# Seven block products for 20 instead of 16 FFN blocks, and two instead of four FFN blocks ahead of the sampled tokens

## The chip, the core and the metric

The kernel runs on one core of a Trainium2 chip. A core has TensorE (PE in the profile; its weight loads are PEld), VectorE (DVE), ScalarE (ACT), GpSimd (POOL) and SyncE (SP), which here only issues DMAs. Each engine works through its own instructions in a fixed order and waits on semaphores. TensorE reads SBUF and accumulates in PSUM, which has eight banks. The metric is the device time of one execution in microseconds (us).

## The reference

One layer of a decoder step for 1024 prompt tokens and 64 sampled tokens (8 sequences of 8), width 1024, all in float32:

```python
shift1, scale1, gate1, shift2, scale2, gate2 = mod
mix, states = mixer(rmsnorm(x, g_mix) * (1 + scale1) + shift1)
x = x + gate1 * (mix @ w_out)
x = x + gate2 * swiglu(rmsnorm(x, g_ffn) * (1 + scale2) + shift2, w_gate_up, w_down)
```

`swiglu` computes `(silu(gate) * up) @ w_down` with 2816 hidden columns. The mixer is a short convolution, a dilated window attention and a window attention; for the sampled tokens it reads key and value caches of up to 2048 positions per sequence. A final RMS norm follows. The outputs are the tokens and the updated caches.

## The kernel before

**Layout.** Activations lie transposed: 128 channels on the partitions, the 1088 tokens along the free axis, in three groups (`GRP`): 366, 366 and 356 tokens. The 64 sampled tokens are the end of the third, "group 2". A row buffer (`row`, 11 of them) holds 128 channels of all tokens, an `act_tile` (3 of them) holds all 1024 channels of one group, split in two halves.

**Every large matmul is three.** To keep float32 accuracy, `halves` (L85) splits a weight tile of 128 x 512 into a high half (ScalarE, L90) and a low half (VectorE, at times GpSimd, L91), and activations are split in the same way. `mm3` (L199) then issues three matmuls for each 128 x 128 block: L205 high by high, L206 high by low, L207 low by high. Weights arrive through SP's queue into five `wraw` buffers and are split into four `wsp` buffers. `gemm` (L217) multiplies one output block: two weight tiles, and for each group 8 x 3 = 24 matmuls.

**The order of the work.** The program is written in one order, and a planner places each instruction on its engine by readiness in its own timing of the program; earlier code has precedence. After the attention of the prompt the code goes on:

- `sample_steps` (L714) is the attention of the sampled tokens. It streams the caches through seven `raw` buffers: scores (L661), minimum, exponential, transposes, weighting of the values (L695). It stops nine times, and at each stop two steps of `ahead_steps` (L879) are issued: splitting the mix of groups 0 and 1, the output projection `w_out` of these groups (eight steps), the norm (`second_rstd`, `second_norm`), then `gate_up` of the FFN blocks 0 to 3 for groups 0 and 1, each with one modulation tile (`late_mod`), and the eight steps of their down projection. Six of these come after the last stop.
- The "mid" stage: the mix of group 2 is split (`split_mix`, L612), `w_out` of group 2 is computed for eight output blocks, then its norm (`rstd` L784, with the broadcast matmuls L801 into a bank of the kind "s"; `second_norm` L810), and `gate_up` of blocks 20 and 21 for groups 0 and 1.
- The "ffn" stage: group 2 of blocks 0 to 3, with one `sums_step` (L955) behind each; their down projection for group 2; then pairs of blocks, (20, 21), (4, 5) and so on to (18, 19), each pair with its down projection into the residual rows `x1` (`add_gated`).
- The tail: the last pair's down projection, the final norm and the output, over other token ranges (`LAST`).

**Seven products.** `gate_up_2x2` (L968) computes gate and up for groups 0 and 1 as one 2 x 2 block product: the weights' blocks are gate and up by the two halves of the 1024 input channels, the activations' blocks the two groups by the same halves. Instead of eight products of blocks it computes seven, from sums of weights (`t1` to `t4`, on GpSimd, four `tw` buffers) and sums of activations (`SA`, made once by four calls of `sums_step`: on GpSimd L947, then VectorE and ScalarE). A product is 4 x 3 = 12 matmuls of 366 columns. Group 2 of the block is multiplied plainly (`third`). Banks: the products take those of the kinds "s" (two) and "t" (two), plain gates those of kind "g" (three).

**Caches.** The updated caches are copied by 38 DMAs, DRAM to DRAM, from ScalarE's queue; `next_copy` issues the next of them behind a given instruction.

## Time and profile before

| | us |
|---|---|
| median of 3 runs | 1411.46 |
| lowest, highest | 1411.25, 1416.62 |
| profiled execution | 1411.32 |
| its span | 1409.5 |

The profile is of one execution. Its span runs from the first instruction of the program to the last; the execution's own time has 1.8 us more around it. A row of a window shows, for each engine, the time it was busy and how many instructions (x) it ran, then the granted share of TensorE's clock, the share of the DMA engines' time and the GB/s moved. Matmuls overlap in the pipeline, so a matmul's own duration is longer than what it adds; the spacing of starts is what counts. A group's row gives line, engine, operation, output and inputs with their shapes, the count, then busy us and mean ns, then the engine's idle time before it and who ended it.

### The profile page before, as it was taken

How to read it: one execution, taken by the hardware profiler on the slowest of the kernel's cores; microseconds unless marked ns; L12 is line 12 of the kernel's file. 1: busy time of each engine (PE TensorE's matmuls, PEld its weight loads, DVE VectorE, ACT ScalarE, POOL GpSimd, SP SyncE). 2: the span in 40 equal slices, each digit the busy share in tenths (PEclk: the TensorE clock that was granted, in tenths of full speed). 3: DMA queues.
4: the chain of work that ended last, by engine and by line, in shares of the span. 5: the costliest groups of instructions: out<-in, count | busy, mean ns of one | idle time of the engine just before them, and what ended most of it. 6: DMA issues, size and time to landing. Idle time of an engine off the chain costs nothing.

```text
span 1409.5 us, 23915 instructions
## 1 busy us (share of the span) xinstructions
PE 1353.3 (96%) x9097; PEld 1286.7 (91%) x9097; DVE 841.0 (60%) x1935; ACT 582.5 (41%) x1204; POOL 329.1 (23%) x364
## 2 busy tenths in 40 slices
PE   7999999999999998998998999999999999999994
PEld 5889999979898887888998999999999999999994
DVE  5468768265775326214569665757565666665657
ACT  5398764465654325222344413131313232322243
POOL 2143343233335220102015020202021111111114
PEclk9999999999999999999999999999999999999997
DMA  9342421452416679875333513141515142423103
GB/s 361 107 160 99 135 99 29 128 191 90 143 31 218 208 251 331 280 253 169 112 123 103 143 45 120 30 165 45 186 31 187 51 159 68 144 87 130 44 30 128
DMA packets 100804, 190.81 MB, mean 135 GB/s; under 512 B 14048, under 2 KB 51456, under 8 KB 100096
## 3 DMA queue, kind: packets, MB, share of 16 engines
q1 hardware_dynamic: 94112, 135.67, 30.1%
q10 hardware_dynamic: 6416, 53.55, 10.6%
q8 instruction: 72, 1.18, 0.3%
q14 instruction: 44, 0.36, 0.1%
q0 software_dynamic: 160, 0.04, 0.0%
HBM read 181.22 MB, written 59.23 MB: 171 GB/s over the span
## 4 chain that ended last, share of the span: by engine, by line
PE 83%; DMA 7%; DVE 4%; issue 2%; POOL 1%; ACT 1%; SPq 0%; POOLq 0%; ACTq 0%; DVEq 0%
PE ps_g L205 18%; PE ps_g L207 18%; PE ps_g L206 18%; PE ps_s L206 3%; PE ps_s L205 3%; PE ps_s L207 3%; DMA wraw<-in_w_gu 3%; PE ps_o L579 3%; PE ps_t L206 2%; PE ps_t L205 2%; PE ps_t L207 2%; PE ps_t L570 2%; DMA raw<-in_bv 1%; PE ps_g L180 1%; PE ps_s L528 1%
## 5 line engine op out<-in xcount | busy, mean ns | idle before, releaser
L205 PE MATMUL ps_g<-act,wsp 128*128 128x366 f32 (+1 forms) x1192 | 400.0, 337 | 5.5 <-ACT wsp L90 3.3
L207 PE MATMUL ps_g<-act,wsp 128*128 128x366 f32 (+1 forms) x1192 | 396.0, 333 | 4.0 <-DVE wsp L91 3.9
L206 PE MATMUL ps_g<-act,wsp 128*128 128x366 f32 (+1 forms) x1192 | 397.7, 334 | 0.4 <-DVE act L617 0.4
L90 ACT ACTIVATE wsp<-wraw 128x512 fp32r<-128x512 f32 x232 | 145.3, 629 | 270.5 <-PE ps_g L207 170.4
L205 PEld LDWEIGHTS ps_g<-act,wsp 128*128 128x128 f32 x1192 | 227.6, 191 | 13.0 <-issue 5.5
L207 PEld LDWEIGHTS ps_g<-act,wsp 128*128 128x128 f32 x1192 | 227.1, 191 | 9.2 <-DVE wsp L91 5.0
L91 DVE TENSOR_TENSOR wsp<-wraw,wsp 128x512 fp32r<-128x512 f32 x194 | 144.5, 745 | 146.3 <-ACT wsp L90 141.5
L206 PEld LDWEIGHTS ps_g<-act,wsp 128*128 128x128 f32 x1192 | 227.8, 191 | 4.0 <-issue 2.5
L205 PE MATMUL ps_g<-hid,wsp 128*128 128x366 f32 (+3 forms) x464 | 152.7, 331 | 4.6 <-DVE ts L767 3.6
L206 PE MATMUL ps_g<-hid,wsp 128*128 128x366 f32 (+3 forms) x464 | 152.3, 328 | 1.7 <-DVE hid L852 1.7
L207 PE MATMUL ps_g<-hid,wsp 128*128 128x366 f32 (+3 forms) x464 | 152.6, 329 | 0.0
L972 POOL TENSOR_TENSOR tw<-wraw 128x512 f32<-128x512 f32 x16 | 21.8, 1365 | 322.9 <-DMA wraw<-in_w_gu 157.0
L205 PEld LDWEIGHTS ps_g<-hid,wsp 128*128 128x128 f32 x464 | 87.6, 189 | 7.2 <-issue 3.6
L90 ACT ACTIVATE wsp<-tw 128x512 fp32r<-128x512 f32 x64 | 40.5, 633 | 122.5 <-PE ps_g L207 59.3
L206 PE MATMUL ps_s<-act,wsp 128*128 128x366 f32 x272 | 90.2, 332 | 0.0
L205 PE MATMUL ps_s<-act,wsp 128*128 128x366 f32 x272 | 90.1, 331 | 0.0
L206 PEld LDWEIGHTS ps_g<-hid,wsp 128*128 128x128 f32 x464 | 87.9, 189 | 2.5 <-DVE hid L852 2.3
L207 PE MATMUL ps_s<-act,wsp 128*128 128x366 f32 x272 | 89.9, 330 | 0.0
L91 POOL TENSOR_TENSOR wsp<-wraw,wsp 128x512 fp32r<-128x512 f32 x38 | 49.9, 1313 | 169.6 <-ACT wsp L90 158.0
L207 PEld LDWEIGHTS ps_g<-hid,wsp 128*128 128x128 f32 x464 | 87.8, 189 | 0.0
L763 DVE SCALAR_TENSOR_TENSOR p_qc<-ps_g,MOD,p_qc 128x366 f32<-128x366 f32 (+3 forms) x99 | 56.5, 572 | 39.9 <-PE ps_g L207 38.0
L763 DVE SCALAR_TENSOR_TENSOR p_q<-ps_g,MOD,p_q 128x366 f32<-128x366 f32 (+3 forms) x99 | 55.3, 570 | 38.5 <-PE ps_g L207 38.5
(346 smaller groups left out, 2453.3 us busy)
## 6 DMA issues: line engine op xcount, KB each, us to landing
wraw<-in_w_gu SPq DMA_DIRECT2D x112, 256.0 KB, 2.7
wraw<-in_wmod SPq DMA_DIRECT2D x64, 256.0 KB, 3.6
raw<-in_bk SPq DMA_DIRECT2D x30, 512.0 KB, 7.8
raw<-in_bv SPq DMA_DIRECT2D x30, 512.0 KB, 8.4
out_bk_b<-in_bk ACTq DMA_DIRECT2D x12, 1016.0 KB, 7.3
wraw<-in_w_in SPq DMA_DIRECT2D x36, 256.0 KB, 5.4
wraw<-in_w_d SPq DMA_DIRECT2D x36, 256.0 KB, 2.6
mraw<-in_wmod SPq DMA_DIRECT2D x32, 256.0 KB, 5.2
```

The lines of the kernel that those rows point to most:

```text
L90: S.activation(sp[:, 0, :], raw, AF.Copy)
L91: (V if not state["sub"] or state["n"] % state["sub"] else G).tensor_tensor(sp[:, 1, :], raw, sp[:, 0, :].bitcast(F32), op=OP.subtract)
L180: ins = PE.matmul(ps[32 * q:32 * q + 32, :256], lhsT=csil[:, 4 * hf + q, :], rhs=raws[2 * hf + q // 2][:, q % 2 * 256:q % 2 * 256 + 256], ...
L205: PE.matmul(ps[:, :n], lhsT=w_hi, rhs=a(0, ak), start=first and j == 0, stop=False, **kw)
L206: PE.matmul(ps[:, :n], lhsT=w_hi, rhs=a(1, ak), start=False, stop=False, **kw)
L207: PE.matmul(ps[:, :n], lhsT=w_lo, rhs=a(0, ak), start=False, stop=last and j == m - 1, **kw)
L528: PE.matmul(ps[:, :sn], lhsT=QH[:, qsl], rhs=KS[hd][:, kk], start=True, stop=False)
L570: PE.transpose(pt[:, col:col + 128], Sb[:, (kb - k0) * 128:(kb - k0 + 1) * 128], ident)
L579: PE.matmul(po[:, q0:q0 + w], lhsT=Vt[:, kb, hd].rearrange("p a b -> p (a b)"), rhs=PT[:, hl, c0:c0 + w], start=fresh, stop=ch is chunks[- ...
L763: ins = V.scalar_tensor_tensor(x1[m][:, c0:c0 + k], ps[:, :k], MOD[:, gate + m, 0:1], x1[m][:, c0:c0 + k], op0=OP.mult, op1=OP.add)
L972: G.tensor_tensor(t1, b12, b11, op=OP.subtract)
```

## The change

`FF_GROUPS` becomes two lists. Ahead of the sampled tokens stand the blocks 0 and 1 only; blocks 2 and 3 join the late pairs, and all late pairs, (20, 21) among them, are computed by seven products.

```diff
-FF_GROUPS = ((0, 4), (20, 2)) + tuple((f, 2) for f in range(4, 20, 2))
+FF_AHEAD = (0,)
+FF_PAIRS = (20,) + tuple(range(2, 20, 2))
```

The down weights are now stored for pairs alone, so the ahead blocks' down projection is four steps of one weight tile instead of eight; with this the ahead steps are 18 instead of 24. The modulation tiles move from the gate steps to every second projection step:

```diff
         for m in range(KC):
             w_out(m, (0, 1))
+            late_mod(m % 2)
             yield
...
-                late_mod(1)
```

The mix of group 2 goes into an `act_tile` instead of a tile of the mid stage, and is split before the memory of the sampled tokens is given back. The early constants' memory is given back before the mid stage, and the buffers of the sums (`tw`, `SA`) are taken from there on:

```diff
+    mx[2] = act_tile()
+    split_mix(2, mx[2])
     samp.close()
...
     early_pool.close()
...
+    sp_ = sums.enter_context(tc.tile_pool(name="sums", bufs=1, reuse_waits="tile"))
```

The mid stage holds the sums and the seven products of blocks 20 and 21, without their group 2 (`hh` is `None`), which stays where it was:

```diff
+        for m in range(KC):
+            w_out(m, (2,))
+            if m % 2:
+                sums_step(m // 2)
+        second_norm(2, second_rstd(2))
+        first = [row("u_ff") for _ in range(NPRE)]
+        for f, u in enumerate(first):
+            gate_up_2x2(FE + f, u, None)
```

In the ffn stage, group 2 of blocks 0 and 1 is computed without sums, and blocks 2 and 3 become the second pair. `gate_up_2x2` issues two cache copies instead of one for the blocks below 6 and in the mid stage:

```diff
+        for _ in range(2 if f < 6 or hh is None else 1):
             next_copy(ins)
```

In the tail, the buffers of the final norm (accumulator, broadcast row, three temporaries) lie in one tile that takes the place of the sum `sa1`, instead of a pool of their own.

More of the change, by code (lines that the diff above doesn't have):

```diff
@@ L912, in _build @@
     late_mod(16)
+    mx[2] = act_tile()
+    split_mix(2, mx[2])
     samp.close()
-    FE = FF_GROUPS[1][0]
-    with tc.tile_pool(name="mid", bufs=1) as mid:
-        scratch["ff"] = mid
-        state["sub"] = 0
-        mx[2] = mid.tile([128, 2, KC, 366], F32R, name="mx2")
-        split_mix(2, mx[2])
-        for m in range(KC):
-            w_out(m, (2,))
-        second_norm(2, second_rstd(2))
-        first = [row("u_ff") for _ in range(NPRE)]
-        for f, u in enumerate(first):
-            gate_up(FE + f, u, None, (0, 1))
@@ new lines, in gate_up_2x2, with product, third @@
+    def gate_up_2x2(f, u, hh):
+        c2, n2 = GRP[2]
+        b11, b12, b22, b21 = [load(d["w_gu"][f, n, hf]) for n, hf in ((0, 0), (1, 0), (1, 1), (0, 1))]
+        t1, t2, t3, t4 = [tw() for _ in range(4)]
+        G.tensor_tensor(t1, b12, b11, op=OP.subtract)
+        G.tensor_tensor(t2, b22, t1, op=OP.subtract)
+        G.tensor_tensor(t3, b22, b12, op=OP.subtract)
+        G.tensor_tensor(t4, b21, t2, op=OP.subtract)
+        uv = row("uv")
+        u2, u3 = uv[:, 0:N2], uv[:, N2:2 * N2]
+        g0, g1, g2 = [u[:, c:c + n] for c, n in GRP]
+        def product(ps, w, a, first):
+            mm3(ps, w, [(k, k) for k in range(4)], a, N2, first=first, more=not first)
+        def third(ps, w, half, first):
+            if hh is not None:
@@ new lines, in gate_up_2x2 @@
+        pd = ps_tile("s")
+        product(pd, wsel(halves(t3)), lambda hl, k: SA[3][:, hl, k, :], True)
+        V.tensor_tensor(u3, u2, pd[:, :N2], op=OP.add)
+        w = wsel(halves(b21))
+        product(pa, w, lambda hl, k: h2[0][:, hl, 4 + k, :], False)
+        ins = S.activation(g0, pa[:, :N2], AF.Silu)
+        third(pg, w, 1, False)
+        if hh is not None:
+            ins = S.activation(g2, pg[:, :n2], AF.Silu)
+        pe = ps_tile("t")
+        product(pe, wsel(halves(t1)), lambda hl, k: SA[1][:, hl, k, :], True)
@@ L1015, in gate_up_2x2 @@
+        V.tensor_tensor(g0, g0, u2, op=OP.mult)
+        if hh is not None:
             split_hid(u, hh, 0, N2)
```

188 lines of the change are left out of this document (81 added, 107 removed).

## The prediction

> **What bounds the kernel now.** I read the page first (engine shares, chain), then the busy time by stage around the places that change, then the rows that price single operations.
>
> ```profile
> span 1409.5 us, 23915 instructions
> PE 1353.3 (96%) x9097; PEld 1286.7 (91%) x9097; DVE 841.0 (60%) x1935; ACT 582.5 (41%) x1204; POOL 329.1 (23%) x364
> ...
> PE 83%; DMA 7%; DVE 4%; issue 2%; POOL 1%; ACT 1%; SPq 0%; POOLq 0%; ACTq 0%; DVEq 0%
> ```
>
> TensorE is the bound: 83% of the chain. The remainder sits in a few stages, so next the stretches from the start of the sampled tokens to the first late pair, and one steady late pair:
>
> ```profile
> core 0: us, PE busy (x) PEld busy (x) DVE busy (x) ACT busy (x) POOL busy (x), PEclk, DMA share, GB/s
> 442.00:546.00 104.00, 97.44 (x1016) 83.34 (x1015) 37.11 (x103) 37.36 (x70) 26.85 (x51) 0.97 0.79 257
> 546.00:650.70 104.70, 96.91 (x815) 86.42 (x813) 29.02 (x61) 29.79 (x53) 10.63 (x10) 0.93 0.78 265
> 650.70:679.30 28.60, 28.60 (x175) 28.54 (x172) 17.25 (x35) 8.66 (x24) 5.58 (x7) 1.00 0.39 116
> 679.30:710.70 31.40, 31.40 (x195) 31.40 (x194) 19.43 (x39) 13.08 (x23) 4.78 (x5) 1.00 0.45 126
> 710.70:744.20 33.50, 33.50 (x205) 33.50 (x205) 21.92 (x64) 16.31 (x34) 7.64 (x12) 1.00 0.38 127
> 744.20:781.80 37.60, 33.74 (x194) 32.85 (x193) 33.21 (x53) 18.61 (x38) 16.10 (x12) 0.95 0.39 112
> ...
> 1156.00:1224.50 68.50, 68.13 (x409) 67.58 (x409) 42.83 (x83) 19.06 (x35) 10.47 (x9) 1.00 0.32 109
> ```
>
> By the code these are: 442 to 650.7 sampled tokens, interleaved with the "ahead" steps; 650.7 to 679.3 the six down steps left of them, under which the mix of group 2 is split; 679.3 to 710.7 the output projection of group 2 (192 matmuls); 710.7 to 744.2 its norm, under which TensorE computes 192 products of blocks 20 and 21; 744.2 to 781.8 group 2 of blocks 0 to 3 (192 matmuls) together with the sums for the seven products; the last row is one pair of late blocks. The price of a matmul is the spacing in an unbroken run:
>
> ```profile
> 569.90 0.33 PE L205 MATMUL ps_g<-act,wsp 128*128 128x366 f32 x1
> ...
> 581.97 0.34 PE L205 MATMUL ps_g<-act,wsp 128*128 128x366 f32 x1
> ```
>
> 72 matmuls lie between these two starts (24 turns of L205, L206, L207), so one of 366 columns costs 12.07/72 = 0.1676 us; one of 356 costs 31.4/192 = 0.1635 (the row at 679.3). From 679.3 to 781.8, 102.5 us pass for 31.4 + 192 x 0.1676 + 31.4 + about 1 (the twelve matmuls of the norm) = 96.0: **6.5 us are lost** there, almost all in the stage with the sums.
>
> **The products.** For groups 0 and 1 a plain block costs 2 x 2 x 8 x 3 = 96 matmuls, the other way 7 x 4 x 3 = 84. Blocks 2, 3, 20 and 21 change over: 48 matmuls fewer, 48 x 0.1676 = **-8.0 us**. The down matmuls stay the same number, and each group's last projection too. Blocks 2 and 3 become a ninth steady pair. By the prices that is 168 x 0.1676 + 96 x 0.1635 + 96 x 0.1676 + 48 x 0.1635 = 67.8 us; the row at 1156 shows 68.5, so a pair loses **+0.7**. Its additional additions into x1 and its weight differences cost nothing beyond that: in that row VectorE is busy 42.8 us and GpSimd 10.5 of 68.5, under TensorE's 68.1.
>
> **The sampled tokens lose cover.** Out of 442 to 679.3 go 2 x 96 gate and up matmuls and 96 of the 192 down ones, 48.3 us of work that fills waits of a stage with a DMA share of 0.78. Out of its DMA go eight loads of 256 KB for the gates, four for the down, and four copies of 1 MB. The sixteen loads of the last four modulation tiles move on SP's queue from the gate steps to the projection steps, 4.2 MB among the caches' loads; at 257/0.79 = 325 GB/s these are 13 us, and the row at 442 leaves 0.21 x 104 = 22 us free. What the stage loses today, by the waits on TensorE:
>
> ```profile
> 614.84 0.67 PE L205 MATMUL ps_g<-act,wsp 128*128 128x366 f32 x1 [3.01 <-ACT wsp L90]
> ...
> 643.19 1.08 PE L695 MATMUL ps_o<-raw,PTs 128*32 128x128 f32 x16 [3.81 <-DMA raw<-in_bv]
> ```
> ```profile
> 614.70:621.50 6.80, 6.62 (x23) 5.45 (x24) 3.33 (x6) 2.31 (x6) 2.54 (x2) 0.50 0.35 117
> ...
> 643.00:648.80 5.80, 5.61 (x31) 5.20 (x32) 0.60 (x1) 0.00 (x0) 0.00 (x0) 0.50 0.63 229
> ```
>
> Each of the two gaps runs into a stretch at half the granted clock (0.50 in the last columns): 6.8 us at half cost 3.4, 5.8 cost 2.9, so the gaps cost 6.4 and 6.7 us. The first belongs to a weight of blocks that leave the stage, so it may vanish (-6.4). On the other side the mix of group 2 gets a new wait: its tile takes the slot of the hidden values of the ahead blocks, so ScalarE's copies stand until the last ahead down matmul has read them, with the weight copies (L90) of the projection behind them, and TensorE behind those. Today 28.6 us of down work hide this split. Its length, from ScalarE's rows:
>
> ```profile
> 658.43 0.43 ACT L616 ACTIVATE mx<-p_qc 128x292 fp32r<-128x292 f32 x1
> 658.76 0.24 ACT L620 ACTIVATE mx<-mixS 128x64 fp32r<-128x64 f32 x1
> ```
>
> 8 x 0.67 = 5.4 us, of which the first projection matmuls can overlap a little; with a cold clock after it 5.4 + 3.4 = 8.8. Between -6.4 and +8.8 I take **0**, a gap gone against a split laid open.
>
> **The sums move into the projection of group 2.** This is the term that decides. The sums' price, from VectorE's and GpSimd's groups in today's place (738.5 to 782):
>
> ```profile
> L953 DVE TENSOR_TENSOR sa<-tw,sa 128x366 fp32r<-128x366 f32 x12 | 8.6, 715 | 0.0
> L958 DVE TENSOR_TENSOR tw<-tw 128x366 f32<-128x366 f32 x4 | 3.6, 912 | 3.9 <-POOL tw L947 3.9
> L953 DVE TENSOR_TENSOR act<-tw,act 128x366 fp32r<-128x366 f32 x4 | 2.9, 724 | 0.0
> L965 DVE TENSOR_TENSOR tw<-tw 128x366 f32<-128x366 f32 x4 | 2.9, 724 | 0.0
> L960 DVE TENSOR_TENSOR tw<-tw 128x366 f32<-128x366 f32 x4 | 2.7, 666 | 0.0
> L962 DVE TENSOR_TENSOR tw<-tw 128x366 f32<-128x366 f32 x4 | 2.1, 527 | 0.0
> ...
> L947 POOL TENSOR_TENSOR tw<-act 128x366 f32<-128x366 f32 x16 | 20.2, 1276 | 10.9 <-DVE tw L962 7.6 <-DVE sa L953 2.8 <-DVE act L953 0.5
> ```
>
> VectorE: 22.8 us; together with the weights' low halves that filled it there (33.21 of 37.6) and TensorE waited for it. In the new order VectorE has, from the first projection matmul to the end of the norm: the projection's 19.4 (row at 679.3), the sums' 22.8, the norm's 21.92 less its gates' part, and for two blocks by seven products seven low halves and seven evacuations each:
>
> ```profile
> L91 DVE TENSOR_TENSOR wsp<-wraw,wsp 128x512 fp32r<-128x512 f32 x7 | 4.8, 689 | 4.3 <-ACT wsp L90 4.3
> L836 DVE TENSOR_TENSOR u_ff<-u_ff,ps_g 128x366 f32<-128x366 f32 x2 | 1.0, 522 | 0.0
> ```
> ```profile
> L91 DVE TENSOR_TENSOR wsp<-tw,wsp 128x512 fp32r<-128x512 f32 x8 | 5.5, 692 | 4.2 <-ACT wsp L90 3.9
> L994 DVE TENSOR_TENSOR uv<-uv,ps_t 128x366 f32<-128x366 f32 x2 | 1.1, 536 | 1.4 <-PE ps_t L207 1.4
> ```
>
> The norm keeps 21.92 - 4.8 - 1.0 = 16.1; the products take 2 x 7 x (0.69 + 0.54) = 17.2. Less four low halves already in the four buffers (2.8): 19.4 + 22.8 + 16.1 + 17.2 - 2.8 = 72.7 us of VectorE against 31.4 + 168 x 0.1676 + 1 = 60.6 of TensorE. So **VectorE becomes the bound of this stretch**, by 12.1 us if it is never idle, 22 if it is busy 88% as in 744 to 782 (33.21/37.6), 6.4 if one of the four sums (5.7) gets done while the mix is split. After it, blocks 0 and 1 have their 96 matmuls of group 2 without sums, and lose nothing. Against today's 6.5 that is 0 to +15.5; head start and idleness have opposite signs, so I take neither: 12.1 - 6.5 = **+5.6**. Two more waits lie inside: the weight differences take the same four buffers as the sums, so GpSimd's first difference stands until the last sum is kept, with the norm's additions behind it in GpSimd's queue; and the norm of group 2 itself waits for no more than before, since its tile is freed by the same projection that feeds it.
>
> **Hidden parts.** The last tile of the tail moves into a sum's buffer: its last reader is a product of block 19, which the block's remaining products and third group cover. The copies come earlier from ScalarE's queue, two a block at first; DMA shares of 0.32 to 0.45 there hold them.
>
> **The sum.** -8.0 + 0.7 + 0 + 5.6 = -1.7 on the profiled execution's 1411.3 (span 1409.5 and 1.8 around it; the median of the runs is 1411.46, so the same): 1409.6, say **1410**.
>
> **Rivals.** (1) *The matmuls are saved and nothing is paid*: the sums slip into VectorE's idle time (11 of 28.6 us at 650.7), the transition stays at 6.5: 1404, and with the first gap gone 1398; middle 1401. For it speaks VectorE's 60% over the whole; against it 72.7 over 60.6 in the one place. (2) *The accumulation banks* (slower): the norm's broadcast row lies in a bank of the kind of which there are two, and now the seven products use both:
>
> ```profile
> L801 PE MATMUL ps_s<-ident,ir_y x26: 270/275/582, 722.6 to 1402.1; 128*128 128x128 f32 x26
> ```
>
> If block 20's products are issued before it, it waits until their first bank is read, four products or 48 x 0.1676 = 8.0 us, and then holds back block 21's two. TensorE, whose cover already is 28.2 instead of 32.2 us for the 33.5 of the norm, idles in one piece and pays half a clock stretch, 3.4: 1409.6 + 8.0 + 3.4 = 1421. It decides as soon as more than 7 us are added. Against it: the planner may place the row first, as it now places the norm amid gates. (3) *The sampled tokens wait on their caches*, with nothing left to issue, and the split lies open with a cold clock behind it: +8.8 in place of 0, 1418.4, and more for each further half-clock stretch, so 1420. (4) *VectorE and GpSimd block each other*:
>
> ```profile
> L953 DVE TENSOR_TENSOR sa<-tw,sa x12: 526/529/1311, 743.6 to 774.5; 128x366 fp32r<-128x366 f32 x12
> ```
>
> a low half takes 0.53 alone and up to 1.31 when GpSimd runs; the sums' share of this is in their price, but eight weight differences now fall beside the norm: 8 x 0.78 = 6.3, 1416. The Trainium skill says in "SBUF — State Buffer", section "Who interferes with whom", that a VectorE instruction with two SBUF inputs and a GpSimd one that reads SBUF exclude each other for the whole instruction. By that rule the additions in the norm are stretched and those that read an accumulation bank are not, so the result is this rival's 1416; the 1311 beside 526 agrees. That the matmuls aren't saved can't be: their number is fixed by the code.
>
> **How the numbers follow.** Forecast 0.34, (1) 0.32, (2) 0.18, (3) 0.07, (4) 0.09. Half a per cent (7.1 us) is about what a measurement here can tell from no change: (1) is faster, 0.32; forecast and (4) the same, 0.43; (2) and (3) slower, 0.25. The range goes from (1) with the gap gone, 1398, to -8.0 + 0.7 + 15.5 + 5.4 = +13.6, 1425; the forecast's own is 1404 to 1418.
>
> **What would show it.** TensorE matmuls 9097 - 48 = 9049. VectorE over 90% busy from the projection of group 2 to its norm, with TensorE waiting there for low halves (L91) some 12 us in all; then a stage without loss for blocks 0 and 1. Wrong would be: VectorE under 80% there; a wait of the norm's row for a bank; a gap over 6 us ahead of the projection of group 2; or a steady pair that no longer takes 68.5 us.

## The result, and the profile after

The changed kernel took 1426.39 us (median of 8 runs, 1422.12 to 1434.31) where the kernel before, run beside it, took 1412.05: a ratio of 1.010, 95% interval 1.0076 to 1.0123. It is slower by about 14 us; 1410 was forecast, and 1426.4 lies 1.4 us beyond the upper end of the range. The profiled execution is the slowest of the eight (1434.31 us), some 8 us above the median. That excess lies outside the stretches that follow: the sampled tokens begin 4.8 us later than before, and behind the third groups of blocks 0 and 1 pass 692.1 us, 3.7 more than the work there explains.

The page after, its counts and the chain of waits:

```profile
span 1432.4 us, 23887 instructions
...
PE 1358.3 (95%) x9049; PEld 1286.7 (90%) x9049; DVE 881.8 (62%) x2003; ACT 584.0 (41%) x1208; POOL 346.3 (24%) x374
...
PE 85%; DVE 7%; issue 3%; DMA 2%; ACT 2%; POOL 1%; SPq 0%; POOLq 0%; ACTq 0%; DVEq 0%
```

The 48 matmuls are gone (9097 to 9049), the DMA's share of the chain fell from 7% to 2%, and VectorE's rose from 4% to 7%. The stretches show where (columns as in the rows of before: us, then busy us of PE, PEld, DVE, ACT, POOL, then clock, DMA share, GB/s):

```profile
446.90:632.30 185.40, 171.48 (x1712) 146.57 (x1710) 69.81 (x172) 59.01 (x112) 32.48 (x58) 0.95 0.80 264
632.30:673.50 41.20, 34.60 (x192) 32.56 (x192) 37.99 (x70) 18.89 (x45) 24.11 (x21) 0.96 0.42 118
673.50:685.20 11.70, 0.03 (x1) 0.00 (x0) 11.70 (x18) 4.18 (x9) 8.69 (x7) 0.71 0.07 22
685.20:722.60 37.40, 33.95 (x168) 32.39 (x169) 29.71 (x74) 18.72 (x39) 13.33 (x14) 0.82 0.42 135
722.60:740.30 17.70, 17.70 (x110) 17.70 (x109) 10.00 (x16) 8.08 (x14) 0.00 (x0) 1.00 0.64 206
```

The first row is the stretch of the sampled tokens: 185.4 us, against 237.2 before (442.1 to 679.3). It became 51.8 us shorter for 48.3 us of work taken out. The second is the projection of group 2: 41.2 us where 31.4 stood before. In the third TensorE does next to nothing, and VectorE is busy for the whole of it. The fourth holds the norm's twelve small matmuls and 156 of the 168 product matmuls of blocks 20 and 21: 37.4 us for 26.1 + 1. The last, the third groups of blocks 0 and 1 with the other twelve product matmuls among them, loses nothing. From 632.3 to 722.6 pass 90.3 us for 58.6 of matmuls: **31.7 us are lost**, against 6.5 before. TensorE's waits there, with the total, the number and the longest:

```profile
PE ps_t L802 <- DVE acc L799: 11.7, 1, 11.7
PE ps_g L208 <- DVE act L623: 4.1, 2, 3.1
PE ps_g L209 <- DVE wsp L93: 2.4, 3, 1.1
PE ps_s L806 <- DVE ir_y L242: 1.4, 1, 1.4
```

L802 is the norm's reduction, which in TensorE's order stands directly behind the projection, ahead of the products; it waits for the last of the norm's additions (L799). L623 is the low half of the mix's sampled columns, L93 a low half of a weight. And the clock, in finer stretches of the same trace:

```profile
668.40:673.40 5.00, 4.06 (x25) 3.60 (x23) 5.00 (x9) 1.54 (x3) 2.91 (x4) 1.00 0.47 132
673.40:678.40 5.00, 0.13 (x1) 0.00 (x0) 5.00 (x7) 1.52 (x3) 3.35 (x3) 1.00 0.05 18
678.40:685.20 6.80, 0.00 (x0) 0.00 (x0) 6.80 (x12) 2.74 (x6) 5.45 (x4) 0.50 0.11 30
685.20:698.80 13.60, 11.76 (x40) 10.81 (x41) 10.77 (x26) 5.39 (x10) 7.40 (x5) 0.50 0.20 62
698.80:705.60 6.80, 5.81 (x34) 5.35 (x32) 5.23 (x18) 5.39 (x13) 2.44 (x4) 1.00 0.58 193
```

5.0 us after the matmuls stop the granted clock is halved, and it stays so for 13.6 us behind the idle piece. TensorE is busy for 11.8 of them, so the half clock costs some 5.9 us. VectorE's groups from 632 to 686 show why the additions are late (count, then busy us and mean ns, then idle before):

```profile
L93 DVE TENSOR_TENSOR wsp<-wraw,wsp 128x512 fp32r<-128x512 f32 x14 | 11.2, 805 | 0.0
L935 DVE TENSOR_TENSOR sa<-tw,sa 128x366 fp32r<-128x366 f32 x12 | 9.3, 781 | 0.0
...
L947 DVE TENSOR_TENSOR tw<-tw 128x366 f32<-128x366 f32 x4 | 3.9, 979 | 0.0
L942 DVE TENSOR_TENSOR tw<-tw 128x366 f32<-128x366 f32 x4 | 3.9, 966 | 0.0
L935 DVE TENSOR_TENSOR act<-tw,act 128x366 fp32r<-128x366 f32 x4 | 2.9, 721 | 0.0
L940 DVE TENSOR_TENSOR tw<-tw 128x366 f32<-128x366 f32 x4 | 2.9, 712 | 0.9 <-POOL tw L929 0.9
L799 DVE TENSOR_TENSOR acc<-acc,tmp 128x356 f32<-128x356 f32 x2 | 2.5, 1274 | 0.0
```

L935 to L947 are the sums. All four steps but for their last two low halves stand in VectorE's queue before the norm's last addition, and of these groups only L940 has idle time before it (0.9 us): VectorE is busy 49.7 of the 52.9 us up to the reduction and is still late. L619 and L623, the low halves of the mix of group 2, take another 8.5 us there; they are not among the rows shown.

### The profile page after: what moved, and what is told of

The parts are those of the page before. It is cut to its first block, busy times and chain, and to the rows that moved or that the text cites. A ratio compares the mean times of both kernels' runs of the same rounds, so it can differ in the third digit from the quotient of the medians.

```text
span 1432.4 us, 23887 instructions
## 1 busy us (share of the span) xinstructions
PE 1358.3 (95%) x9049; PEld 1286.7 (90%) x9049; DVE 881.8 (62%) x2003; ACT 584.0 (41%) x1208; POOL 346.3 (24%) x374
## 4 chain that ended last, share of the span: by engine, by line
PE 85%; DVE 7%; issue 3%; DMA 2%; ACT 2%; POOL 1%; SPq 0%; POOLq 0%; ACTq 0%; DVEq 0%
PE ps_g L207 17%; PE ps_g L208 17%; PE ps_g L209 17%; PE ps_s L207 4%; PE ps_s L208 4%; PE ps_s L209 4%; PE ps_t L207 3%; PE ps_t L208 3%; PE ps_t L209 3%; PE ps_o L581 2%; PE ps_t L572 2%; PE ps_g L182 1%; PE ps_s L663 1%; PE ps_s L530 1%; PE ps_o L697 1%
## 5 line engine op out<-in xcount | busy, mean ns | idle before, releaser
L207 PE MATMUL ps_g<-act,wsp 128*128 128x366 f32 (+1 forms) x1096 | 367.7, 337 | 3.3 <-DVE u L330 2.6
L208 PE MATMUL ps_g<-act,wsp 128*128 128x366 f32 (+1 forms) x1096 | 364.7, 333 | 4.6 <-DVE act L623 4.1
L209 PE MATMUL ps_g<-act,wsp 128*128 128x366 f32 (+1 forms) x1096 | 362.3, 332 | 2.6 <-DVE wsp L93 2.4
L92 ACT ACTIVATE wsp<-wraw 128x512 fp32r<-128x512 f32 x218 | 136.7, 629 | 260.2 <-PE ps_g L209 152.2
L207 PEld LDWEIGHTS ps_g<-act,wsp 128*128 128x128 f32 x1096 | 208.9, 191 | 11.6 <-issue 5.9
L208 PEld LDWEIGHTS ps_g<-act,wsp 128*128 128x128 f32 x1096 | 209.0, 191 | 9.0 <-DVE act L623 4.7
L209 PEld LDWEIGHTS ps_g<-act,wsp 128*128 128x128 f32 x1096 | 208.0, 190 | 6.0 <-DVE wsp L93 3.9
L93 DVE TENSOR_TENSOR wsp<-wraw,wsp 128x512 fp32r<-128x512 f32 x186 | 138.2, 744 | 118.4 <-ACT wsp L92 113.5
L207 PE MATMUL ps_g<-hid,wsp 128*128 128x366 f32 (+3 forms) x496 | 164.0, 333 | 4.3 <-DVE ts L769 3.4
L208 PE MATMUL ps_g<-hid,wsp 128*128 128x366 f32 (+3 forms) x496 | 164.3, 331 | 1.9 <-DVE hid L857 1.9
L209 PE MATMUL ps_g<-hid,wsp 128*128 128x366 f32 (+3 forms) x496 | 163.7, 330 | 0.0
L955 POOL TENSOR_TENSOR tw<-wraw 128x512 f32<-128x512 f32 x20 | 27.4, 1372 | 358.0 <-DMA wraw<-in_w_gu 189.0
L207 PE MATMUL ps_s<-act,wsp 128*128 128x366 f32 x336 | 112.3, 334 | 1.6 <-ACT u_ff L985 1.0
L208 PE MATMUL ps_s<-act,wsp 128*128 128x366 f32 x336 | 111.9, 333 | 0.0
L209 PE MATMUL ps_s<-act,wsp 128*128 128x366 f32 x336 | 111.6, 332 | 0.0
L92 ACT ACTIVATE wsp<-tw 128x512 fp32r<-128x512 f32 x80 | 50.6, 632 | 142.8 <-PE ps_g L209 65.5
L207 PEld LDWEIGHTS ps_g<-hid,wsp 128*128 128x128 f32 x496 | 94.1, 190 | 7.6 <-issue 3.6
L208 PEld LDWEIGHTS ps_g<-hid,wsp 128*128 128x128 f32 x496 | 94.4, 190 | 3.4 <-DVE hid L857 3.1
L209 PEld LDWEIGHTS ps_g<-hid,wsp 128*128 128x128 f32 x496 | 94.3, 190 | 0.0
L207 PE MATMUL ps_t<-sa,wsp 128*128 128x366 f32 x240 | 80.5, 335 | 0.0
```

The lines of the kernel that those rows point to most:

```text
L92: S.activation(sp[:, 0, :], raw, AF.Copy)
L93: (V if not state["sub"] or state["n"] % state["sub"] else G).tensor_tensor(sp[:, 1, :], raw, sp[:, 0, :].bitcast(F32), op=OP.subtract)
L207: PE.matmul(ps[:, :n], lhsT=w_hi, rhs=a(0, ak), start=first and j == 0, stop=False, **kw)
L208: PE.matmul(ps[:, :n], lhsT=w_hi, rhs=a(1, ak), start=False, stop=False, **kw)
L209: PE.matmul(ps[:, :n], lhsT=w_lo, rhs=a(0, ak), start=False, stop=last and j == m - 1, **kw)
L955: G.tensor_tensor(t1, b12, b11, op=OP.subtract)
```

## The experiments

The first theory (A): VectorE has more work than TensorE beside the projection because of the sums, its queue is in order, and so the norm's additions and with them TensorE's reduction are late. Against it: it is TensorE's order alone (B), the seven products of blocks 20 and 21 and their operands (C), or the stretch of the sampled tokens (D). Ratios are to the kernel before, run beside each; the changed kernel has 1.0100. The runs called "no sums" leave out the sums' arithmetic, and "sums on GpSimd only" VectorE's part of it, so their seven products multiply other operands; TensorE's work is the same. Blocks 20 and 21 of the second run read the half of group 1's activations that the sums had overwritten, so their values differ from the reference's there; the work is the same.

| run | us, median | ratio, 95% |
|---|---|---|
| changed kernel | 1426.4 | 1.0100 (1.0076 to 1.0123) |
| no sums | 1416.2 | 1.0039 (1.0022 to 1.0055) |
| blocks 20, 21 plain | 1416.5 | 1.0031 (1.0007 to 1.0055) |
| late sums, 18 blocks | 1404.4 | 0.9959 (0.9944 to 0.9974) |
| block 20 first | 1425.1 | 1.0111 (1.0076 to 1.0145) |
| no sums, block 20 first | 1402.8 | 0.9958 (0.9935 to 0.9981) |
| sums on GpSimd only | 1414.6 | 1.0035 (1.0015 to 1.0055) |
| 18 blocks, mix early | 1416.9 | 1.0054 (1.0032 to 1.0075) |
| before, sums spread | 1409.5 | 0.9998 (0.9978 to 1.0018) |
| before, no sums | 1404.6 | 0.9955 (0.9937 to 0.9972) |
| 18 blocks, mix early, no sums | 1403.6 | 0.9942 (0.9921 to 0.9963) |
| late sums, mix's halves shared | 1405.8 | 0.9957 (0.9940 to 0.9974) |
| block 20 first, half of the low halves on GpSimd | 1425.1 | 1.0095 (1.0073 to 1.0117) |
| block 20 first, six buffers | 1425.0 | 1.0110 (1.0094 to 1.0126) |
| changed kernel, six buffers | 1436.2 | 1.0188 (1.0168 to 1.0209) |
| late sums, six buffers | 1413.7 | 1.0032 (1.0015 to 1.0049) |

### Without the sums

```diff
-        a21, a22, a11 = whole(h2[1], k), whole(h2[1], k + 4), whole(h2[0], k)
-        V.tensor_tensor(a22, a21, a22, op=OP.add)
-        keep(1, k, a22)
...
+        for i in (1, 2, 4):
+            for x in range(2):
+                S.activation(SA[i][:, x, k, :], h2[0][:, x, k, :].bitcast(F32), AF.Copy)
```

> The changed kernel without the arithmetic of the sums: in each of the four steps only six copies on ScalarE fill the three tiles, and VectorE's 22.8 us and GpSimd's 20.2 us of sums are gone, so the seven products multiply wrong operands; everything on TensorE keeps its number and order. The sums make VectorE the bound of the stretch (theory A): from the start of the projection of group 2 (632.3 in the changed kernel's trace) to the third groups of blocks 0 and 1 (722.6) pass 90.3 us for 60.6 us of matmuls; without the sums VectorE has 72.7 - 22.8 = 49.9 us of work there, less than TensorE, so the 11.7 us of idleness before the norm's reduction shrink to 5 or less, the 20.5 us at half clock with them, and the time falls from 1426 by 15 to 23 us to 1403 to 1411. The seven products of blocks 20 and 21 are to blame, not the sums (theory C): the stretch loses 20 us or more as before, 1421 to 1428. The loss lies in the sampled tokens or in the copy of the mix (theory D): no gain, 1421 to 1428.

1.0100 became 1.0039: 8.6 us were won, of the 15 to 23 that theory A expected. Stretches of this run, from the projection to the end of the third groups:

```profile
632.00:666.70 34.70, 32.69 (x192) 31.22 (x192) 24.39 (x52) 23.85 (x59) 13.08 (x12) 1.00 0.50 150
666.70:672.70 6.00, 0.06 (x1) 0.00 (x0) 4.28 (x7) 2.61 (x5) 4.51 (x4) 0.85 0.28 80
672.70:686.00 13.30, 12.15 (x60) 11.54 (x60) 8.35 (x26) 5.66 (x13) 3.29 (x4) 0.81 0.08 20
```

The projection fell from 41.2 to 34.7 us and the idle piece from 11.7 to 6.0, with VectorE no longer full (24.4 of 34.7, 4.3 of 6.0). So VectorE was the bound there; but an idle piece of 6 us stays, with a part of the slow clock behind it. Only its last 1.2 us are the norm's last square and addition. Before them VectorE still has two weights' low halves for the products in its queue (0.93 and 0.86 us) and waits 1.08 us for ScalarE ahead of the first; the last gated addition, behind both, ends at 671.6. So a part of it is the products' own operands (C), and nothing on TensorE stands under it. ScalarE has more to do in this run, since copies fill the tiles (23.9 us in the projection against 18.9), so 8.6 us is if anything too little for the sums.

### Blocks 20 and 21 plain

```diff
         for f, u in enumerate(first):
-            gate_up_2x2(FE + f, u, None)
+            gate_up(FE + f, u, None, (0, 1))
```

> The changed kernel with blocks 20 and 21 computed plainly ahead of group 2's norm (24 matmuls more, 4.0 us); the sums stay in the projection of group 2. Theory A (the sums): VectorE still has the projection's 19.4 and the sums' 22.8 us before it can finish the norm's additions, so TensorE idles before the norm's reduction about as long, 8 to 12 us; behind it there are 32.2 us of plain gate matmuls with less VectorE work, which may win 2 to 5 back: 1421 to 1430 in all. Theory C (the seven products: their low halves, weight differences on GpSimd and their evacuations fill VectorE): the stretch loses 8 us at most, 1406 to 1413. Theory D (sampled tokens): 1426 + 4 = 1430.

1.0031, so 9.7 us were won in spite of 24 more matmuls: between what A and what C expected. Plain gates need no sums, so 54 of their matmuls stand ahead of the reduction in TensorE's order and cover the norm's way. But the reduction comes as late as before (680.7 us, 52 behind the first projection matmul), because the sums still hold VectorE.

### Late sums, eighteen blocks

```diff
             gate_up(f0 + f, u, None, (2,))
...
+            sums_step(f)
...
                 gate_up(f, u, hh, (2,))
+                sums_step(f - FE + 2)
```

These calls replace those in the projection, and blocks 20 and 21 are plain.

> The changed kernel with blocks 20 and 21 computed plainly, and the four sum steps moved out of the projection of group 2: one behind the third groups of each of blocks 0 and 1, one behind each of those of blocks 20 and 21 (18 blocks by seven products, still two blocks ahead of the sampled tokens). Theory A: nothing but the plain work stands beside the projection, which then takes 31 to 34 us, and the norm 34 to 36, as in the kernel before; the sums lie beside 62.8 us of third groups and cost 3 us at most. Against the kernel before: 24 matmuls fewer (-4.0), the first gap of the sampled tokens gone or not (-3.6 to 0), the transition's 6.5 us down to about 3: 1399 to 1407. Theory C gives the same here. Theory D (the loss lies ahead of the projection): 1418 or more.

0.9959: this version beats both kernels, the one before by 0.4% (0.26 to 0.56). The stretches of its projection, norm and third groups, and the first operation of its four sum steps (shortest, median and longest ns, then first and last start):

```profile
630.20:666.70 36.50, 32.29 (x192) 31.38 (x193) 34.63 (x68) 18.22 (x42) 19.05 (x18) 1.00 0.45 131
666.70:700.20 33.50, 33.50 (x206) 33.50 (x205) 24.03 (x68) 19.02 (x38) 7.73 (x12) 1.00 0.48 152
700.20:716.00 15.80, 15.80 (x99) 15.80 (x98) 15.52 (x25) 9.14 (x18) 4.63 (x4) 1.00 0.34 87
```
```profile
L940 DVE TENSOR_TENSOR tw<-tw x4: 527/530/1269, 641.8 to 705.3; 128x366 f32<-128x366 f32 x4
```

The planner took two of the late steps and a part of the third forward into the projection all the same (641.8 on) and left the rest for the end of the norm and behind it, the last step at 705.3. That is what VectorE can carry: 34.6 of 36.5 us. Norm and third groups lose nothing. What is lost is 5 us in the projection, 4.1 of them waits for the mix's low halves (L623).

### Block 20 first

```diff
-        second_norm(2, second_rstd(2))
         first = [row("u_ff") for _ in range(NPRE)]
-        for f, u in enumerate(first):
-            gate_up_2x2(FE + f, u, None)
+        gate_up_2x2(FE, first[0], None)
+        second_norm(2, second_rstd(2))
+        gate_up_2x2(FE + 1, first[1], None)
```

> The changed kernel with the seven products of block 20 issued in the code ahead of group 2's norm, so that they stand before the norm's reduction in TensorE's fixed order. Theory B (it is only the order that makes TensorE idle in one piece): the 11.7 us of idleness are filled with block 20's products and the clock stays up, 1408 to 1414. Theory A (VectorE has more work than TensorE in the stretch): VectorE's additions and low halves for block 20 now stand ahead of the norm's, the idleness moves behind block 20, and at most the half-clock stretch is shorter: 1418 to 1428.

1.0111, as the changed kernel. Two waits of this run show where the idle piece went:

```profile
PE ps_t L207 <- ACT wsp L92: 8.8, 1, 8.8
...
ACT wsp L92 <- POOL tw L955: 2.9, 1, 2.9
```

Block 20's second product now waits 8.8 us, for a weight difference that GpSimd makes behind the sums. Order alone is worth nothing (B falls) as long as the sums are there.

### Without the sums and block 20 first

The two edits above together.

> As the run without the sums' arithmetic (the sums' tiles filled by six copies a step on ScalarE, products of wrong operands), and block 20's seven products issued in the code ahead of group 2's norm, so that in TensorE's order 72 products stand before the norm's reduction and 24 between it and the broadcast row, where the run without the sums has 0 and 12. That run took 1416.2 us and lost 94.0 - 76.3 = 17.7 us between the start of the projection and the end of the third groups of blocks 0 and 1: 6.2 us idle before the reduction, 2.7 and 1.0 us before products behind it, and 0.84 of the clock for 33 us. Theory E (with VectorE relieved, what is left is TensorE's order: nothing stands under the 6 us that the norm takes from the last gated addition to the reduction): the idle piece and the half clock vanish, 1404 to 1409. Theory C (the products' own operands are late: weight differences on GpSimd, low halves on VectorE): TensorE waits at block 20's second product instead and the time stays within 3 us of 1416.

0.9958: 11.4 us less than without the sums alone. Its stretches:

```profile
627.10:661.70 34.60, 32.59 (x193) 31.35 (x194) 24.28 (x52) 23.85 (x59) 13.15 (x12) 1.00 0.49 153
661.70:696.60 34.90, 33.23 (x199) 32.31 (x199) 31.26 (x79) 22.15 (x44) 11.00 (x13) 1.00 0.53 192
696.60:709.50 12.90, 12.90 (x81) 12.90 (x80) 7.61 (x13) 6.32 (x12) 0.69 (x2) 1.00 0.47 141
```

72 products stand under the norm's way, the clock stays at 1.00, and from 627.1 to 709.5 pass 82.4 us for 76.3. Read with the three runs before it, the four cells are: sums and norm first 1.0100; sums and block 20 first 1.0111; no sums, norm first 1.0039; neither 0.9958. The sums cost 8.6 us in the one order and 21.6 in the other, the order 11.4 us without the sums and nothing with them. Either of the two alone suffices to stop TensorE.

### The sums' additions on GpSimd only

```diff
-        for i in (1, 2, 4):
+        for i, t in ((1, whole(h2[1], k)), (2, whole(h2[1], k + 4)), (4, whole(h2[0], k)), (4, whole(h2[0], k + 4))):
             for x in range(2):
-                S.activation(SA[i][:, x, k, :], h2[0][:, x, k, :].bitcast(F32), AF.Copy)
+                S.activation(SA[i][:, x, k, :], t, AF.Copy)
```

> As the run without the sums' arithmetic, but with the sixteen additions on GpSimd kept (20.9 us in the changed kernel); ScalarE copies their results into the sums' tiles, and VectorE has none of the sums' work (products of wrong operands again). TensorE's order is that of the changed kernel. It measures rival 4 by itself, GpSimd's work beside VectorE. If VectorE's additions are held while GpSimd adds (in the changed kernel VectorE was busy 57.2 us from 632 to 686 where the same instructions at their undisturbed durations are 39.9), the low halves and the norm's additions are stretched by 8 to 15 us in all and the time comes out 3 to 8 us over that of the run without the sums (1416.2): 1419 to 1424. If they aren't held, 1415 to 1418.

1.0035 against 1.0039: GpSimd's additions beside the norm cost nothing that these intervals (2.8 us to each side of the one) can show. Low halves of weights (L93) and the mix's (L623) from 630 to 711, first without any sums, then with GpSimd's:

```profile
L93 DVE TENSOR_TENSOR wsp<-wraw,wsp 128x512 fp32r<-128x512 f32 x22 | 17.5, 810 | 3.8 <-ACT wsp L92 3.6
...
L623 DVE TENSOR_TENSOR act<-mixS,act 128x64 fp32r<-128x64 f32 x8 | 2.5, 341 | 0.0
```
```profile
L93 DVE TENSOR_TENSOR wsp<-wraw,wsp 128x512 fp32r<-128x512 f32 x23 | 19.0, 844 | 0.7 <-ACT wsp L92 0.7
...
L623 DVE TENSOR_TENSOR act<-mixS,act 128x64 fp32r<-128x64 f32 x8 | 4.8, 631 | 0.0
```

VectorE's instructions do get longer (L623 from 341 to 631 ns), but VectorE has idle time here and takes it up (it is busy 35.6 of the 42.0 us up to the reduction). The run doesn't say what the same stretch costs where VectorE is full. The rule of the Trainium skill ("SBUF — State Buffer", section "Who interferes with whom") is seen in the instructions, not in the time.

### Eighteen blocks, the transition as before

The late-sums kernel, with the mix of group 2 in a tile of the "mid" pool and the sums' pool opened only behind it:

```diff
-    mx[2] = act_tile()
-    split_mix(2, mx[2])
...
+        mx[2] = mid.tile([128, 2, KC, 366], F32R, name="mx2")
+        split_mix(2, mx[2])
```

> Eighteen blocks by seven products and two FFN blocks ahead of the sampled tokens, but the transition as it was before: the mix of group 2 has a tile of its own and is split under the last ahead work, blocks 20 and 21 are plain, and the sums' tiles open only after the norm of group 2, so that all four steps stand beside the third groups of blocks 0, 1, 20 and 21 (in the run with late sums 2.5 of the four steps still got into the projection, and the split lay open: 4.7 us of waits of TensorE). Theory A (the place of VectorE's work decides): the projection takes 31 to 33 us, no loss in the norm, the sums cost 0 to 4 us beside 62 us of third groups; against the run with late sums (1404.4) 2 to 6 us less, 1398 to 1403. If the split's place doesn't matter, or the sums cost as much beside the third groups, 1404 to 1408.

1.0054, a miss: 13 us more than with the sums half in the projection. The stretches after the norm, and the sums' first operation:

```profile
660.90:694.50 33.60, 33.60 (x207) 33.60 (x206) 21.90 (x65) 17.53 (x35) 7.69 (x12) 1.00 0.39 126
694.50:712.20 17.70, 16.15 (x97) 15.56 (x97) 17.70 (x26) 9.00 (x20) 10.02 (x8) 1.00 0.29 80
712.20:732.00 19.80, 12.21 (x51) 10.51 (x50) 17.75 (x43) 6.87 (x14) 6.41 (x4) 0.74 0.29 88
```
```profile
L951 DVE TENSOR_TENSOR tw<-tw x4: 527/906/1297, 690.9 to 718.0; 128x366 f32<-128x366 f32 x4
```

The planner ran all four steps in one piece from 690.9 on, though the code has them behind four different groups. The evacuations of the third groups (L841) and the hidden values of the down projection (L1037) queue behind them (TensorE waits 3.2 us for the first and 3.0 for the second), and the clock falls to 0.74. The place had changed, not the mechanism.

### Before, with the sums spread

In the kernel before, the four calls moved to other groups:

```diff
-                sums_step(f)
+                if f % 2:
+                    sums_step(f // 2)
...
+                    sums_step(f - FE + 2)
```

> The kernel before with its sums spread: the four steps that stood behind each of the third groups of blocks 0 to 3 now stand behind those of blocks 1, 3, 20 and 21; nothing else changes. The kernel before lost 6.5 us there, of which 4.4 were waits of TensorE beside the sums, with VectorE busy 33.2 of 37.6 us. Theory A (VectorE's work of 37 us in a stretch of 31 us of TensorE): the loss shrinks by 3 to 6 us, 1405 to 1409. If that loss has another cause, 1410 to 1413.

0.9998: nothing. But the sums didn't move either. The row of their first operation, in the kernel before and in this one:

```profile
L958 DVE TENSOR_TENSOR tw<-tw x4: 526/910/1302, 740.5 to 766.9; 128x366 f32<-128x366 f32 x4
```
```profile
L958 DVE TENSOR_TENSOR tw<-tw x4: 528/910/1304, 736.1 to 762.5; 128x366 f32<-128x366 f32 x4
```

26.4 us from the first to the last in both, in a trace that is 4.4 us earlier at this point. The planner places them by readiness, so this run tells nothing on its question.

### Before, without the sums

The edit of the first run, in the kernel before.

> The kernel before without the arithmetic of the sums (six copies a step on ScalarE fill the tiles, products of wrong operands). It measures what the sums cost in their old place: by the profile 6.5 us were lost from the end of the norm to the end of the third groups of blocks 0 to 3. If these are the sums' (VectorE busy 33.2 of 37.6 us there), the time falls by 4 to 6.5 us, to 1404 to 1407; if not, 1409 to 1412. In the changed kernel the sums cost 9.2 us with the norm's reduction first (1425.5 against 1416.2) and 22 with block 20 first (1425.1 against 1402.8).

0.9955: 6.4 us, the 6.5 that the prediction read from the profile. Projection, norm and third groups of blocks 0 to 3:

```profile
675.30:706.70 31.40, 31.40 (x194) 31.40 (x193) 19.42 (x39) 13.09 (x23) 4.77 (x5) 1.00 0.43 126
706.70:740.30 33.60, 33.60 (x207) 33.60 (x206) 18.82 (x61) 21.06 (x48) 3.60 (x8) 1.00 0.38 126
740.30:771.70 31.40, 31.40 (x194) 31.40 (x193) 15.03 (x24) 16.26 (x33) 0.00 (x0) 1.00 0.44 133
```

TensorE is without a gap: the whole loss of before in these stretches was the sums'.

### Eighteen blocks without the sums

The edit of the first run, in the kernel with the transition as before.

> The run with eighteen blocks and the mix early, without the arithmetic of the sums (products of wrong operands). That run took 1416.9 us and lost 2 us in the projection, nothing in the norm, and 13.9 us from 694 to 732, where all four steps of sums stood in one piece and TensorE waited for VectorE. Theory A (VectorE's queue is in order: a block of sums delays what TensorE needs next, wherever it stands): without them 1402 to 1405. If the loss had another cause (the sampled tokens, the missing 24 matmuls' cover), 1412 or more. It is also a look at what two FFN blocks ahead instead of four do to the sampled tokens by themselves: against the kernel before without sums it has 24 matmuls fewer (-4.0 us) and the ninth pair's 0.7, so anything above that run's time minus 3 is what the lost cover costs.

0.9942, so the sums cost 15.8 us in that place. Against the run before it (0.9955) the gain is 1.8 us, where 24 matmuls less (4.0) and the ninth pair's 0.7 make 3.3. The difference of 1.5 us is within the intervals, so no cost of the lost cover of the sampled tokens is shown.

### The mix's small halves shared

```diff
-                V.tensor_tensor(dst[:, 1, k, m:n], mixs[k], dst[:, 0, k, m:n].bitcast(F32), op=OP.subtract)
+                eng(MIXE[k]).tensor_tensor(dst[:, 1, k, m:n], mixs[k], dst[:, 0, k, m:n].bitcast(F32), op=OP.subtract)
```

> The run with late sums (18 blocks, 1404.4 us), with one change: in the split of group 2's mix the low halves of the 64 sampled columns are made by the engine that makes the chunk's other low half (GpSimd for four of eight), not all by VectorE. In that run TensorE waited 4.1 us for these low halves at the start of the projection. If VectorE's queue is what is late there, 1 to 3 us fewer: 1401.5 to 1403.5; if GpSimd's operations (0.7 us and more each) are as late, 1404 to 1406.

0.9957: no gain over 0.9959 that could be measured; the intervals allow one of 1 to 3 us. The trace shows that the edit did what it was for: TensorE's wait for the low halves fell from 4.1 us to 1.1. So VectorE's queue did make them late, but from the first projection matmul to the reduction the time fell only from 42.7 to 41.6 us.

### Half of the low halves on GpSimd

Block 20 first, and in `keep`:

```diff
-        V.tensor_tensor(lo, t, hi.bitcast(F32), op=OP.subtract)
+        (V if i in (1, 2) else G).tensor_tensor(lo, t, hi.bitcast(F32), op=OP.subtract)
```

> The changed kernel with block 20's products ahead of the norm, and of the sums' sixteen low halves eight moved from VectorE to GpSimd; all results as in the reference. With block 20 first, the sums cost 22.3 us (1425.1 with them, 1402.8 without); GpSimd's share of them cost nothing by itself beside the norm-first order (1414.6 against 1416.2). Theory A (VectorE's share of the sums holds the norm and the products): VectorE loses 8 x 0.78 = 6.2 us of its 22, so 4 to 8 us are won, 1417 to 1421. If GpSimd's queue is the one that holds (the weight differences of block 20 stand behind the sums there), the time rises: 1425 to 1432.

1.0095 against 1.0111: at most a fraction of the 4 to 8 us expected. Block 20's second product waits 8.5 us here, as long as before. The stretch from the first projection matmul to the reduction, with block 20 first and then in this run:

```profile
628.20:692.60 64.40, 48.20 (x251) 45.34 (x252) 61.27 (x96) 28.64 (x62) 41.89 (x33) 0.87 0.34 102
631.00:698.20 67.20, 49.03 (x251) 46.13 (x252) 61.95 (x87) 28.64 (x62) 48.22 (x41) 0.87 0.32 98
```

VectorE has nine instructions fewer (96 to 87) and is busy as long (61.3 and 62.0 us), because the others take longer, beside a GpSimd that is busy 48.2 us instead of 41.9: the last addition of a sum step (L947) took 529 ns in the median before and takes 1118 here. The result spoke for another theory (F): not the amount of VectorE's work, but the sums' chain from GpSimd over VectorE, ScalarE and VectorE again, held up by the four `tw` buffers, at whose end the weight differences stand. Three runs with six buffers were made for it.

### Six buffers

```diff
-        return sp_.tile([128, 512], F32, tag="tw", bufs=4, name="tw")
+        return sp_.tile([128, 512], F32, tag="tw", bufs=6, name="tw")
...
-            t = cst.tile([128, NS], F32, tag="ts", bufs=2, name="ts")
+            t = cst.tile([128, NS], F32, tag="ts", bufs=1, name="ts")
```

> The changed kernel with block 20's products ahead of the norm, and six tw buffers instead of four (for their room one of two small ts buffers goes, written and read in VectorE's own order). The work on every engine is the same as in the run with block 20 first (1425.1). Theory A (amount of VectorE's work): within 3 us of it, 1422 to 1428. Theory F (the sums' chain through four buffers, with the weight differences at its end): the sums end some 8 us earlier than at 678, the 8.8 us wait of block 20's second product goes down by most of that, 1410 to 1418.

> The changed kernel with six tw buffers instead of four and one ts buffer instead of two, nothing else. Theory A: 1423 to 1428 as the changed kernel. Theory F: the sums end earlier than at 684, the norm's additions on VectorE behind them too, and of the 11.7 us of idleness before the norm's reduction 3 to 6 us go, with part of the half-clock stretch: 1416 to 1421.

> The run with late sums (18 blocks, blocks 20 and 21 plain; 1404.4 us) with six tw buffers and one ts buffer. Its sums cost next to nothing already, so both theories give 1402 to 1406; a planner that now gets a third whole step into the projection, ahead of the norm, could cost 2 to 5 us, 1406 to 1409.

F falls. With block 20 first the 8.8 us wait does go down, to 2.4, as F expected, but the time doesn't (1.0110 against 1.0111): other waits grow (for L623 from 2.6 to 5.6 us), and VectorE is busy 61.7 of 64.4 us up to the reduction, as with four buffers; the changed kernel is 12 us slower with the additional buffers (1.0188), the late sums 10 us (1.0032 against 0.9959). TensorE's longest waits in the changed kernel with six buffers:

```profile
PE ps_t L802 <- DVE acc L799: 18.7, 1, 18.7
PE ps_g L208 <- DVE act L623: 5.6, 2, 4.7
```

With more buffers the last two low halves of the sums and two low halves of weight differences for the products also stand ahead of the norm's last addition in VectorE's queue. Up to the reduction VectorE is busy 57.4 of 60.9 us (91 instructions) where it was 49.7 of 52.9 (87), and the reduction waits 18.7 us instead of 11.7. It is the time that VectorE needs for what stands ahead of the norm that decides, as theory A says.

## Why the prediction was wrong

**Matmuls.** 9049, as said. **The ninth pair** cost what was said: in the late-sums kernel 688.4 us pass from 716.0 to the end of the span, and 627.7 (781.8 to 1409.5 before) less 48 down matmuls of 0.1635 plus 68.5 is 688.4. In the changed kernel the time from one pair's first product to the next pair's is 67.7 to 70.0 us.

**The sampled tokens.** Taken as 0 between -6.4 and +8.8. The stretch became 3.5 us shorter than its work explains. That is within the scatter of the profiles: from the first scores to the projection pass 221.8 to 228.7 us in the kernel before and its two variants, 175.9 to 179.8 in the others. The split laid open costs 4.1 us of waits for VectorE's low halves and 0.5 for ScalarE's copies at the head of the projection, and a half-clock stretch of 3.4 us (640.8 to 644.2), some 1.7: 6.3 in all, against 8.8. Together that is near the 0, but partly by luck: the 3.0 us wait for a weight went as hoped, while one of 5.6 us came (L686, for ScalarE's L676), and the split was held by VectorE, not by ScalarE's copies. Rival 3 fell.

**The sums: the step that failed.** The forecast said that VectorE becomes the bound of the stretch, and that is what happened: 38.0 of 41.2 us and then 11.7 of 11.7. Its size was wrong. It set VectorE's 72.7 us against all of TensorE's 60.6 and took the difference, 12.1, as the loss, taking VectorE to be never idle. But TensorE's 28.2 us of products could not stand beside that work: they come after the reduction in TensorE's order, and four of the seven need the sums. Before the reduction VectorE had 37.99 + 11.70 = 49.7 us to do and TensorE only the projection's 31.4. From 632.3 to 685.2 pass 52.9 us, so 21.5 are lost; behind it 37.4 pass for 27.1, so 10.2 more, some 5.9 of them the clock's. That makes the 31.7. The 72.7 was also too small: VectorE was busy 79.4 of the 90.3 us, and the low halves of the mix (8.5), which the split's new place puts into the projection, were not in the sum. Where VectorE was relieved and products stood under the norm, the run without sums and with block 20 first, the stretch came down to 6 us of loss.

The prediction's upper bound for this term, +15.5, was VectorE at 88% of its time, again over the whole stretch; VectorE did come out at 88% (79.4 of 90.3), but with more work. Measured, the term is 31.7 - 6.5 = 25.2 us, of which the 6.3 of the split are counted above already: 18.9 where 5.6 stood. With the matmuls, the pair and the sampled tokens, -8.0 + 0.7 - 3.5 + 25.2 = +14.4, and the medians differ by 14.3, where -1.7 was forecast. The clock stretch was priced only in rivals and bounds.

**What was to show it.** VectorE over 90% was right up to the reduction (92% and 100%), but over the whole stretch it is 88%. The stage of blocks 0 and 1 loses nothing, as said. "Some 12 us of waiting for low halves (L91)" was wrong: 2.4 us were for low halves of weights (now L93), 11.7 in one piece for the norm's additions.

**The rivals.** (1) Nothing paid, 1401: that is where the run without sums and with block 20 first came out, 1402.8. It needs both. And even it is no better than the kernel before without its sums (0.9958 and 0.9955): of 7.3 us saved, 6 go in the transition, 3.2 of them because the projection takes 34.6 us with the split laid open. (2) The accumulation banks: the broadcast row waited 1.4 us, and for VectorE's `ir_y`, not for a bank. The mechanism was wrong, though its price, an idle piece with a cold clock behind it, was of the kind that came. (4) VectorE and GpSimd: the run with GpSimd's additions alone shows no loss, but there VectorE had idle time. In the changed kernel it had almost none. The durations of its instructions from the projection to the reduction add up to 56.6 us, and to 39.1 if each is put at the shortest that its kind has in the trace (instructions overlap a little, so the first is more than the 49.7 us of busy time). So a good part of VectorE's lateness is that its instructions take longer there. That this is GpSimd's doing fits the run with eight low halves on GpSimd, in which VectorE's busy time didn't fall. The rival priced it at 6.3 us, for the eight weight differences alone. A run with VectorE's sums and without GpSimd's was not made, so its share of the loss is not known.

**What stays open.** The loss is the sums', and VectorE's queue carries it; how much of VectorE's time there is the number of its instructions and how much their stretch beside GpSimd isn't separated. Computing the sums under the sampled tokens, where VectorE is idle for 116 of 185 us, wasn't tried: the sums' pool opens only when the pools of that stretch are closed.

## What to carry to other kernels

Set an engine's work against that part of the bounding engine's work which can really stand beside it in the order of its queue, up to the next point where the one waits for the other, and not against the sum of a stage. A gap of that kind has to be priced in one piece, with the clock that it costs. Where a planner orders the queues, moving a call in the code or giving it more buffers is no experiment until the trace shows that the instructions moved, and more buffers can make it slower, because more early work gets ahead of what is urgent.

## What the runs showed of the hardware

The granted clock fell to half 5.0 us after the last matmul and came back only 13.6 us after the matmuls had begun again, though TensorE was busy for 11.8 of these. The prediction had taken one stretch of 6.8 us. In three stretches of 3.41 us in a row (685.20 to 695.44) TensorE was busy 3.02, 2.66 and 2.72 us, and the clock stayed at 0.50; behind the next one, in which it was busy without a gap (695.44 to 698.85), the clock was back. In the run without sums the clock fell 4.2 us after the last matmul (666.7 to 670.9), with TensorE busy 1.49 us of the next 3.42, and was back at 677.7, behind the first 3.41 us without a gap. The Trainium skill ("TensorE: Matmul & The Clock Gate", section "What's actually happening") gives about 3.4 us for an idle window and, of sustained work, for a busy one. Both traces agree with that: the long half clock of the changed kernel goes with waits of 0.3 and 1.4 us in the work behind the idle piece. How full a window has to be, no run here settles.
